# A two-layer diffusion block on one core: the first Hyena butterfly moves into the matmuls, and a third of the modulation product moves between the layers

## The chip, the cores and the metric

The kernel runs on one NeuronCore of a Trainium2 chip. The time is the device time of one execution, in microseconds; a profile of one execution goes with it. The engines are TensorE (PE; its weight loads are listed apart as PEld), VectorE (DVE), ScalarE (ACT), GpSimd (POOL) and SyncE (SP), which issues most of the transfers. Each engine runs its own instructions in order and waits on semaphores for the others.

## The reference, cut to what matters

```python
for l in range(2):                         # 1024 tokens x 1024 channels
    sh1, sc1, g1, sh2, sc2, g2 = _adaln(c, w_mod[l], b_mod[l], 6)   # silu(c) @ w_mod[l] + b_mod[l]
    hl = rmsnorm(xl, norm1_g[l]) * (1 + sc1) + sh1
    if l == 0: yl = _even_mixer(hl, ...)   # RG-LRU heads and Hyena channels
    else:      yl = _conformer_conv(hl, ...)
    xl = xl + g1 * yl
    xl = xl + g2 * _ec_moe(rmsnorm(xl, norm2_g[l]) * (1 + sc2) + sh2, ...)   # 16 experts, 128 tokens each
return rmsnorm(xl, final_g)

def hyena(v, gates):                       # 512 channels, two orders
    z = v
    for o in range(2):
        z = gates[o] * (irfft(rfft(z, 2n) * kf[o], 2n)[:n] + z * bias[o])
```

`w_mod[l]` is 1024 x 6144. Of layer 1, the first third (`sh1`, `sc1`) is wanted by the norm that opens the layer; `g1`, `sh2`, `sc2`, `g2` are wanted after its convolution.

## The kernel before, in words

A tile framework traces the program, orders each engine's instructions ahead of time by a planner (program order as the priority, its own costs for when an input will be ready), and sets the semaphores. On the chip that order is fixed: an engine, or SP's queue of transfers, that waits holds up what stands behind it.

**Stages, in the order of time.** Filters of the Hyena part; input norm and the RG-LRU part; from about 270 to 556 us the Hyena part; output projection, routing and 16 experts of layer 0 (up to about 1279 us); the conformer part of layer 1, which begins with reading the residual stream `acc` back; routing and 16 experts of layer 1.

**Hyena.** Four blocks of 128 channels, two orders each, so eight jobs. A job is a transform of length 2048 as a product with cosines and sines (`G`, 128x128 pieces, float32) for eight token residues, followed by an eight-point transform on DVE. `short` is a block of the input projection, 48 float32r matmuls of 512 columns through `mm3` (a hi/lo split), and a three-tap convolution: three for each channel block. `to_tok` transposes a signal into `ut` (token order) by 8 TensorE transposes and two ACT copies. `hy_fwd` (L593) makes 16 matmuls of 128 columns; the profile counts two records for each float32 matmul. Residues a and a+4 lie beside each other in a PSUM tile; ACT copies one of them to SBUF (`y4`, L596) and `hy_st1` forms sum and difference on DVE (L603, L604). `hy_mid` is all DVE: eight-point transform (`fft8`), product with the filter `K`, first inverse butterfly, eight-point transform back. `hy_inv` (L632) has 16 matmuls; `hy_gate` (L640) multiplies the PSUM result with the gate, reading and writing SBUF in strides of eight elements. The result of order 0 goes through `to_tok` into the job of order 1 of the same block; `X` has three buffers, `ut` two, PSUM four one-bank tiles ("n") and two two-bank tiles ("w", for `short`).

**Modulation.** `silu(c) @ w_mod` is 48 pieces of 1 MB: `ada_load` brings one into the ring `wr` (four buffers, shared with `K` and others), `ada_mm` (L229) multiplies it in four column strips, and after eight pieces `ada_end` transposes the sums (L245), adds the bias and stores rows to DRAM for later. Eight pieces are multiplied during the filters; the other 40 by `self.fill(5)` twice for each channel block, 10 pieces a block.

**Experts.** Each of 192 weight pieces of 1 MB is loaded into `wr` or the ring `wx` (12 buffers, pool `px`), split hi/lo by ACT and DVE (L158, L159) and multiplied. `moe_load` is called after each piece; when the list is empty (the last 20 calls) it does nothing. At the end of expert 15 the result is scaled (L1313) and scattered into `acc` by an indirect transfer from POOL's queue (L1314); then SP loads `acc` in eight tiles (L286) for the conformer's norm, whose outputs `hh`, `hl` lie where `wx` was.

Of the kernel before, what the change touches and what calls it, by code (L numbers as in the profile page):

```python
# [29 lines left out]

VEC = {}
_off = 0
for _n, _w in (("c", 8), ("cc", 8), ("n1g0", 8), ("n1g1", 8), ("n2g0", 8), ("n2g1", 8),
               ("bm0", 48), ("bm1", 48), ("caw", 16), ("cab", 4), ("lbr", 8), ("lbi", 8),
               ("lam", 8), ("cbw", 36), ("cbb", 12), ("fb1", 1), ("fb2", 1), ("fq", 2),
               ("cfb1", 16), ("lng", 8), ("lnb", 8)):
    if _n == "cfb1":
        NLATE = _off
    VEC[_n] = (_off, _w)
    _off += _w  # L40
NVEC = _off
NX = 12
# [7 lines left out]
def layout(inp):  # L50
# [13 lines left out]
    for l in range(2):  # L64
        put(f"n1g{l}", _cols(inp["norm1_g"][l]))
        put(f"n2g{l}", _cols(inp["norm2_g"][l]))
        put(f"bm{l}", _cols(inp["b_mod"][l]))
    put("caw", np.concatenate([_cols(inp["conv_a_w"][0][k]) for k in range(4)], 1))
    put("cab", _cols(inp["conv_a_b"][0]))
    put("lbr", _cols(inp["lru_br"][0]))  # L70
# [75 lines left out]
class Builder:  # L146
# [22 lines left out]
    def consts(self):  # L169
        nc, tc, A = self.nc, self.tc, self.A  # L170
        P, T = self.P, self.T
        self.vec = self.E.tile([128, NLATE], F32, name="vec")
        nc.sync.dma_start(self.vec, A["vec"][:, :NLATE])
        self.idn = P.tile([128, 128], F32, name="idn")
        nc.gpsimd.memset(self.idn, 0.0)
        nc.gpsimd.affine_select(self.idn, self.idn, pattern=[[-1, 128]], compare_op=OP.not_equal,
                                fill=1.0, base=0, channel_multiplier=1)
        self.stack = P.tile([128, NE], F32, name="stack")
        nc.vector.tensor_tensor(self.stack, self.idn[:, 0:NE], self.idn[:, 32:32 + NE], op=OP.add)
        for g in (64, 96):  # L180
# [24 lines left out]
        nc.vector.tensor_scalar(th, th, 0.5, 0.5, op0=OP.mult, op1=OP.add)  # L205
        self.sp = self.E.tile([128, 8, 32], F32, name="sp")
        nc.vector.memset(self.sp, 0.0)
        for i in range(2):
            nc.vector.tensor_tensor(self.sp[:, :, i], th[:, 8 * i:8 * i + 8], self.v("c", 8 * i, 8), op=OP.mult)
        self.mod = [P.tile([128, 48], F32, name=f"mod{l}") for l in range(2)]  # L210
        self.modc = P.tile([128, 16], F32, name="modc")
        self.gg = [[P.tile([128, 8], F32, name=f"gg{l}{i}") for i in range(2)] for l in range(2)]
        self.ggc = P.tile([128, 8], F32, name="ggc")

    def ada_load(self):
        if self.ada_todo:
# [5 lines left out]
    def ada_mm(self):  # L222
        if not self.ada_have:
            return
        l, s, kc, w = self.ada_have.pop(0)
        if kc == 0:
            self.ada_q = self.ps.tile([128, 512], F32, name="q", tag="n")
        for j in range(4):
            self.nc.tensor.matmul(self.ada_q[32 * j:32 * j + 32, :], self.sp[:, kc, :], w[:, j * 512:(j + 1) * 512],  # L229
                                  start=kc == 0, stop=kc == 7, tile_position=(0, 32 * j))  # L230
        if kc == 7:
            self.ada_end(l, s, self.ada_q)

    def fill(self, n=1):
        for _ in range(n):
# [2 lines left out]

    def ada_end(self, l, s, q):
        nc = self.nc  # L240
        r = self.wr.tile([128, 512], F32, name="w", tag="w")
        nc.scalar.copy(r, q)
        t = self.ps.tile([128, 512], F32, name="t", tag="n")
        for b in range(4):
            nc.tensor.transpose(t[:, b * 128:(b + 1) * 128], r[:, b * 128:(b + 1) * 128], self.idn)  # L245
        tv = t.rearrange("p (b j x) -> p j b x", b=4, j=4, x=32)
        nc.vector.tensor_tensor(self.mod[l][:, s * 16:(s + 1) * 16].rearrange("p (j b) -> p j b", j=4),
                                tv[:, :, :, 0], self.v(f"bm{l}", s * 16, 16).rearrange("p (j b) -> p j b", j=4),
                                op=OP.add)
        if l == 0 and s == 0:  # L250
            nc.vector.tensor_tensor(self.modc.rearrange("p (j b) -> p j b", j=4),
# [332 lines left out]
    def hy_fwd(self, p, J):  # L584
        nc = self.nc
        J["K"] = K = self.wr.tile([128, 8, 2, 128], F32, name="w", tag="w")
        nc.sync.dma_start(K, self.kd[J["o"]][J["qd"]])
        J["q"] = []
        for a in range(4):
            q = self.ps.tile([128, 2, 2, 128], F32, name="q", tag="n")  # L590
            for j in range(2):
                for ri in range(2):
                    nc.tensor.matmul(q[:, j, ri], self.G[:, a + 4 * j, ri * 128:ri * 128 + 128], J["u"][:, a + 4 * j],  # L593
                                     start=True, stop=True)
            y4 = p.tile([128, 2, 128], F32, name="y4", tag="y4", bufs=2)
            nc.scalar.copy(y4, q[:, 1])  # L596
            J["q"].append((q, y4))

    def hy_st1(self, p, J):
        V = self.nc.vector  # L600
        J["pq"] = pq = p.tile([128, 8, 2, 128], F32, name="pq", tag="X", bufs=3)
        for a, (q, y4) in enumerate(J["q"]):
            V.tensor_tensor(pq[:, a], q[:, 0], y4, op=OP.add)  # L603
            V.tensor_tensor(pq[:, 4 + a], q[:, 0], y4, op=OP.subtract)  # L604

    def hy_mid(self, p, J):
        V = self.nc.vector
# [27 lines left out]
    def hy_gate(self, p, J):  # L635
        dst = p.tile([128, D], F32, name="zt", tag="zt", bufs=1)
        zv = dst.rearrange("q (p a) -> q a p", a=8)
        gv = J["gate"].rearrange("q (p a) -> q a p", a=8)
        for h, q in enumerate(J["r"]):
            self.nc.vector.tensor_tensor(zv[:, h * 4:h * 4 + 4], q, gv[:, h * 4:h * 4 + 4], op=OP.mult)  # L640
        return dst

    def to_tok(self, src, dst):
        nc = self.nc
        for h in range(2):
            q = self.ps.tile([128, 4, 128], F32, name="q", tag="n")
            for j in range(4):
                a = h * 4 + j
                nc.tensor.transpose(q[:, j], src[:, a::8], self.idn)
            nc.scalar.copy(dst[:, h * 4:h * 4 + 4, :], q)  # L650

    def even_mixer(self, st, so):
        nc, tc, A = self.nc, self.tc, self.A
# [1 line left out]
        def pool(st, name, side=None):  # L655
            return st.enter_context(tc.tile_pool(name=name, bufs=1, side=side, reuse_waits="tile"))

        self.ada_todo = [(l, s_, k) for l in range(2) for s_ in range(3) for k in range(8)]
        self.ada_have = []
        with ExitStack() as s1, ExitStack() as sl:  # L660
            sl.push(self.stE.pop_all())
# [108 lines left out]
                return y  # L770

            def tok(y):
                ut = py.tile([128, 8, 128], F32, name="ut", tag="u", bufs=2)
                self.to_tok(y, ut)
                return ut

# [13 lines left out]
            for i in range(4):  # L790
                J0 = dict(o=0, qd=i, u=tok(short(i)))
                if i == 0:
                    with tc.issue_after(getattr(gload, "ins", gload)):
                        nc.sync.dma_start(self.IG, A["IG"])
                        self.fill(5)
                else:
                    self.fill(5)
                self.hy_fwd(py, J0)
                self.hy_st1(py, J0)
# [4 lines left out]
                self.fill(5)  # L804
# [4 lines left out]
                self.hy_st1(py, J1)  # L809
                self.hy_mid(py, J1)  # L810
                pend.append(J1)
            for _ in range(len(self.ada_todo) + len(self.ada_have)):
                self.fill()
            for ct in (2, 3):
                gate(py, ct, "cv", D)
            sl.close()
# [353 lines left out]

    def moe_load(self, eng=None):
        if not self.names:
            return
        n = 47 * 4 - len(self.names)
        if n % (NX + 4) < 4:
            w = self.wr.tile([128, 2, D], F32, name="w", tag="w")
# [15 lines left out]
    def experts(self, l):  # L1192
        nc, tc, A = self.nc, self.tc, self.A
        V = nc.vector
        with tc.tile_pool(name=f"pe{l}", bufs=1, side="right", reuse_waits="tile") as pe:
# [92 lines left out]
            for e in range(NE):  # L1288
# [20 lines left out]
                if l == 1 and e == NE - 1:  # L1309
# [3 lines left out]
                V.scalar_tensor_tensor(yo, y, self.gates[:, e:e + 1], g2b, op0=OP.mult, op1=OP.mult)  # L1313
                self.last = nc.gpsimd.indirect_dma_start(self.acc[l][:, :], bass.IndirectOffsetOnAxis(ap=xT[e][1][:, 0:1], axis=0),  # L1314
                                             yo, None, compute_op=OP.add)

    def conformer(self, st):
        nc, tc, A = self.nc, self.tc, self.A
# [324 lines left out]
```

## Time and profile before

| | |
|---|---|
| median of 3 runs | 2297.8 us (2295.29 to 2300.59) |
| profiled execution, its own time | 2297.13 us |
| span of its profile | 2295.1 us |
| mean granted TensorE clock | 0.962 of full speed |
| busy share of the span | PE 93%, DVE 79%, ACT 52%, POOL 6% |
| transfers | 616.13 MB, 268 GB/s over the span |

Busy PE time is modelled and overlaps from one matmul to the next, so 93% is no measure of free room; the idle time before an instruction, and what ended it, is. The chain of waits follows the work that ended last back from the end of the span.

### The profile page before, as it was taken

To read this page: it belongs to the slowest core of one execution; us is meant where nothing else is said; L and a number is where in the kernel's file an instruction comes from. 1 tells how busy PE (TensorE), PEld (TensorE's weight loads), DVE (VectorE), ACT (ScalarE), POOL (GpSimd) and SP (SyncE) were. 2 spreads that over 40 slices of the span, in tenths; PEclk is the share of its full clock that TensorE was granted. 3 is DMA by queue.
4 is the path that set the end of the run, shared out by engine and by line. 5 is a ranking of instruction groups with operands and counts; after the bars stand their busy time and mean duration, and the time that the engine had idled before them with its cause. 6 is when DMAs were issued, how large, how long until landed. Compare 5 with 4: busy or idle time off the path is not lost.

```text
span 2295.1 us, 29201 instructions
## 1 busy us (share of the span) xinstructions
PE 2123.7 (93%) x10882; PEld 1654.9 (72%) x10882; DVE 1819.8 (79%) x2876; ACT 1201.7 (52%) x1458; POOL 127.1 (6%) x128
## 2 busy tenths in 40 slices
PE   7999998996968999999999699979689999999997
PEld 5976766775745877877878488867457777777775
DVE  5979799998596988989888533276968898888887
ACT  3658511212214777777777521134247667676774
POOL 0000000000001000000000100010010000000001
PEclk9999999998988999999999899979789999999999
DMA  7241585564848999999998345234779999999974
GB/s 277 107 138 47 198 296 196 220 254 150 291 171 323 368 393 378 379 388 376 391 378 267 105 131 163 93 128 177 257 291 360 384 367 386 368 372 380 365 270 156
DMA packets 210023, 616.13 MB, mean 268 GB/s; under 512 B 27988, under 2 KB 76758, under 8 KB 200089
## 3 DMA queue, kind: packets, MB, share of 16 engines
q1 hardware_dynamic: 198634, 572.85, 66.3%
q0 software_dynamic: 11248, 41.42, 7.2%
q8 instruction: 85, 1.39, 0.2%
q14 instruction: 56, 0.46, 0.1%
HBM read 558.62 MB, written 55.61 MB: 268 GB/s over the span
## 4 chain that ended last, share of the span: by engine, by line
PE 77%; DVE 14%; DMA 3%; issue 3%; ACT 2%; POOL 1%; SPq 0%; POOLq 0%; ACTq 0%; DVEq 0%
PE P L153 20%; PE P L155 20%; PE P L154 19%; PE P L1251 6%; PE q L1216 2%; PE q L593 1%; PE q L229 1%; PE q L394 1%; PE q L510 1%; PE q L632 1%; PE q L1381 1%; PE q L307 1%; POOL rs L278 1%; DVE mm L873 0%; DMA xs<-h2d,ix 0%
## 5 line engine op out<-in xcount | busy, mean ns | idle before, releaser
L159 DVE TENSOR_TENSOR e<-wx,e 128x1024 fp32r<-128x1024 f32 x516 | 619.0, 1221 | 93.1 <-ACT e L158 78.5
L158 ACT CAST e<-wx 128x1024 fp32r<-128x1024 f32 x516 | 539.8, 1051 | 233.9 <-PE P L155 232.1
L153 PE MATMUL P<-e,th 128*128 128x512 f32 x1384 | 562.8, 407 | 0.2 <-ACT th L158 0.2
L155 PE MATMUL P<-e,tl 128*128 128x512 f32 x1384 | 543.5, 393 | 1.6 <-DVE tl L159 1.6
L154 PE MATMUL P<-e,th 128*128 128x512 f32 x1384 | 543.0, 392 | 0.0
L153 PEld LDWEIGHTS P<-e,th 128*128 128x128 f32 x1384 | 260.0, 188 | 61.6 <-issue 7.2
L154 PEld LDWEIGHTS P<-e,th 128*128 128x128 f32 x1384 | 260.1, 188 | 61.0 <-DVE e L159 4.3
L155 PEld LDWEIGHTS P<-e,tl 128*128 128x128 f32 x1384 | 259.7, 188 | 61.5 <-DVE tl L159 2.5
L159 DVE TENSOR_TENSOR e<-w,e 128x1024 fp32r<-128x1024 f32 x176 | 211.8, 1221 | 49.2 <-ACT e L158 29.6
L153 PE MATMUL P<-hh,wh 128*128 128x512 f32 x576 | 229.0, 399 | 7.9 <-DVE y L769 4.2
L158 ACT CAST e<-w 128x1024 fp32r<-128x1024 f32 x176 | 184.1, 1051 | 94.2 <-PE P L155 76.1
L154 PE MATMUL P<-hl,wh 128*128 128x512 f32 x576 | 228.1, 396 | 0.8 <-DVE ms L276 0.8
L155 PE MATMUL P<-hh,wlo 128*128 128x512 f32 x576 | 227.6, 395 | 0.0
L153 PEld LDWEIGHTS P<-hh,wh 128*128 128x128 f32 x576 | 108.8, 189 | 40.4 <-issue 13.2
L154 PEld LDWEIGHTS P<-hl,wh 128*128 128x128 f32 x576 | 109.0, 189 | 28.1 <-issue 5.1
L155 PEld LDWEIGHTS P<-hh,wlo 128*128 128x128 f32 x576 | 108.5, 188 | 27.0 <-issue 4.8
L1314 POOL DMA_INDIRECT acc<-yo,ix x31 | 50.6, 1634 | 934.7 <-DVE yo L1313 934.7
L159 DVE TENSOR_TENSOR tl<-q,th 128x512 fp32r<-128x512 f32 x128 | 84.6, 683 | 7.1 <-ACT th L158 5.1
L158 ACT CAST wh<-w 128x1024 fp32r<-128x1024 f32 x16 | 16.7, 1049 | 136.6 <-PE P L154 124.1
L1251 PE MATMUL P<-wx,xf 128*128 128x512 f32 x176 | 79.1, 592 | 0.0
L158 ACT CAST th<-q 128x512 fp32r<-128x512 f32 x128 | 71.7, 586 | 1.9 <-PE q L1216 1.9
L278 POOL TENSOR_TENSOR rs<-ms,nh 128x1 f32<-128x1 f32 x42 | 23.9, 570 | 830.1 <-issue 435.2
(406 smaller groups left out, 3057.8 us busy)
## 6 DMA issues: line engine op xcount, KB each, us to landing
wx<-i_exp_w SPq DMA_DIRECT2D x272, 1024.0 KB, 7.9
w<-i_exp_w SPq DMA_DIRECT2D x96, 1024.0 KB, 8.1
w<-i_w_mod SPq DMA_DIRECT2D x48, 1024.0 KB, 7.2
wst<-i_w_in SPq DMA_DIRECT2D x20, 512.0 KB, 3.9
kd<-w SPq DMA_DIRECT2D x8, 1024.0 KB, 5.0
w<-kd SPq DMA_DIRECT2D x8, 1024.0 KB
acc<-res SPq DMA_DIRECT2D x16, 512.0 KB, 3.0
e<-i_exp_w SPq DMA_DIRECT2D x16, 512.0 KB, 7.2
```

The lines of the kernel that those rows point to most:

```text
L153: t.matmul(o, lh, rh, start=start, stop=False)
L154: t.matmul(o, lh, rl, start=False, stop=False)
L155: t.matmul(o, ll, rh, start=False, stop=stop)
L158: self.nc.scalar.copy(hi, src)
L159: self.nc.vector.tensor_sub(lo, src, hi.bitcast(F32))
L229: self.nc.tensor.matmul(self.ada_q[32 * j:32 * j + 32, :], self.sp[:, kc, :], w[:, j * 512:(j + 1) * 512], start=kc == 0, stop=kc == 7, ti ...
L278: nc.gpsimd.tensor_tensor(r, m, self.nh[:, :n], op=OP.pow)
L307: nc.tensor.transpose(q[:, t * 128:(t + 1) * 128], x[:, c * 128:(c + 1) * 128], self.idn)
L394: nc.tensor.matmul(q[:, j], h2[:, a + j], ws[:, o, i, cs], start=True, stop=True)
L1216: nc.tensor.transpose(q[:, j], src[:, c * 128:(c + 1) * 128], self.idn)
L1251: nc.tensor.matmul(P[:, ns], f[:, k], h[:, ns], start=k == 0, stop=k == 7)
L1314: self.last = nc.gpsimd.indirect_dma_start(self.acc[l][:, :], bass.IndirectOffsetOnAxis(ap=xT[e][1][:, 0:1], axis=0), yo, None, compute_op ...
```

## The change

1. `hy_st1` and `y4` go. `to_tok` also writes the negative of residues 4 to 7 (one more ACT instruction); `ut` grows from 8 to 12 residues and has one buffer instead of two. `hy_fwd` now makes sum and difference inside PSUM: each matmul has 256 columns, the first with the residue a repeated (stride 0), the second with a+4 and its negative; ACT copies the four PSUM tiles whole to `pq`.
2. `hy_gate` copies the PSUM result by ACT into token order (strided writes), then DVE multiplies it with the gate in one contiguous 128x1024 instruction.
3. The last 16 of the modulation's 48 pieces (layer 1, thirds 1 and 2) leave the Hyena part (`fill(3)` instead of `fill(5)`). They are loaded into `wx` by the `moe_load` calls that did nothing, and multiplied after expert 15 of layer 0. Small vectors move between pools for that.

```diff
-        self.modc = P.tile([128, 16], F32, name="modc")
+        self.sp1 = P.tile([128, 8], F32, name="sp1")
+        nc.vector.tensor_copy(self.sp1, self.sp[:, :, 0])
+        self.modc = self.E.tile([128, 16], F32, name="modc")
...
     def ada_mm(self):
+        sp = self.sp1[:, kc:kc + 1].to_broadcast([128, 32]) if l and s else self.sp[:, kc, :]
         for j in range(4):
-            self.nc.tensor.matmul(self.ada_q[32 * j:32 * j + 32, :], self.sp[:, kc, :], w[:, j * 512:(j + 1) * 512],
+            self.nc.tensor.matmul(self.ada_q[32 * j:32 * j + 32, :], sp, w[:, j * 512:(j + 1) * 512],
...
+    def ada_late(self):
+        if self.moe_l or not self.ada_todo:
+            return
+        l, s, kc = self.ada_todo.pop(0)
+        w = self.px.tile([128, 2048], F32, name="wx", tag="wx", bufs=NX)
+        self.nc.sync.dma_start(w, self.A["w_mod"][l, kc * 128:(kc + 1) * 128, s * 2048:(s + 1) * 2048])
+        self.ada_have.append((l, s, kc, w))
...
     def hy_fwd(self, p, J):
-        J["q"] = []
+        J["pq"] = pq = p.tile([128, 8, 2, 128], F32, name="pq", tag="X", bufs=3)
+        u = J["u"]
         for a in range(4):
             q = self.ps.tile([128, 2, 2, 128], F32, name="q", tag="n")
-            for j in range(2):
-                for ri in range(2):
-                    nc.tensor.matmul(q[:, j, ri], self.G[:, a + 4 * j, ri * 128:ri * 128 + 128], J["u"][:, a + 4 * j],
-                                     start=True, stop=True)
-            y4 = p.tile([128, 2, 128], F32, name="y4", tag="y4", bufs=2)
-            nc.scalar.copy(y4, q[:, 1])
-            J["q"].append((q, y4))
-    def hy_st1(self, p, J):
-            V.tensor_tensor(pq[:, a], q[:, 0], y4, op=OP.add)
-            V.tensor_tensor(pq[:, 4 + a], q[:, 0], y4, op=OP.subtract)
+            for ri in range(2):
+                rs = slice(ri * 128, ri * 128 + 128)
+                nc.tensor.matmul(q[:, :, ri], self.G[:, a, rs], u[:, a:a + 1].to_broadcast([128, 2, 128]),
+                                 start=True, stop=False)
+                nc.tensor.matmul(q[:, :, ri], self.G[:, a + 4, rs], u[:, a + 4:a + 9:4], start=False, stop=True)
+            nc.scalar.copy(pq[:, a:a + 5:4], q)
...
     def hy_gate(self, p, J):
         for h, q in enumerate(J["r"]):
-            self.nc.vector.tensor_tensor(zv[:, h * 4:h * 4 + 4], q, gv[:, h * 4:h * 4 + 4], op=OP.mult)
+            self.nc.scalar.copy(zv[:, h * 4:h * 4 + 4], q)
+        self.nc.vector.tensor_tensor(dst, dst, J["gate"], op=OP.mult)
...
     def to_tok(self, src, dst):
             nc.scalar.copy(dst[:, h * 4:h * 4 + 4, :], q)
+            if h:
+                nc.scalar.activation(dst[:, 8:12, :], q, AF.Identity, bias=0.0, scale=-1.0)
...
-                ut = py.tile([128, 8, 128], F32, name="ut", tag="u", bufs=2)
+                ut = py.tile([128, 12, 128], F32, name="ut", tag="u", bufs=1)
...
-                self.fill(5)          # twice for each channel block
+                self.fill(3)
...
+            self.ada_todo = [(1, s_, k) for s_ in (1, 2) for k in range(8)]   # after the Hyena part
...
     def moe_load(self, eng=None):
         if not self.names:
-            return
+            return self.ada_late()
...
     def experts(self, l):             # after the last expert
+            if l == 0:
+                while self.ada_have or self.ada_todo:
+                    self.ada_late()
+                    self.ada_mm()
```

## Rows read from the trace of the kernel before

**Rows 1.** Windows of the Hyena part: us, busy time (instructions) by engine, clock, DMA.
```profile
268.00:530.00 262.00, 247.50 (x1467) 178.42 (x1466) 236.76 (x421) 50.73 (x81) 0.00 (x0) 0.99 0.66 243
...
360.00:378.00 18.00, 10.26 (x59) 4.28 (x58) 18.00 (x29) 2.51 (x3) 0.00 (x0) 0.81 0.54 184
...
530.00:556.00 26.00, 8.03 (x39) 6.98 (x40) 21.54 (x30) 9.28 (x8) 0.00 (x0) 0.67 0.59 205
```
**Rows 2.** Waits of PE, 268 to 530 us: total, times, longest.
```profile
PE P L153 <- DVE y L769: 4.2, 1, 4.2
PE q L229 <- DMA w<-i_w_mod: 2.6, 2, 1.4
...
PE q L265 <- DVE mod L247: 1.4, 1, 1.4
```
**Rows 3.** Groups by shape, 265 to 560 us: busy us, mean ns, idle before.
```profile
L640 DVE TENSOR_TENSOR zt<-q,y 128x512 f32<-128x512 f32 x16 | 17.9, 1128 | 10.0 <-PE q L632 9.9
...
L603 DVE TENSOR_TENSOR pq<-q,y 128x256 f32<-128x256 f32 x32 | 13.4, 418 | 18.3 <-ACT y L596 17.7
...
L619 DVE TENSOR_TENSOR pq<-pq,sub 128x1024 f32<-128x1024 f32 x8 | 9.8, 1219 | 0.0
...
L650 ACT COPY ut<-q 128x512 f32<-128x512 f32 x16 | 9.1, 588 | 46.5 <-PE q L649 46.5
```
**Rows 4.** Groups by shape of PE, 150 to 240 us: float32 matmuls of two widths.
```profile
L510 PE MATMUL q<-xa,bd 128*128 128x512 f32 x64 | 30.3, 594 | 0.0
...
L510 PE MATMUL q<-xa,bd 128*128 128x256 f32 x32 | 9.9, 389 | 1.5 <-DVE xa L498 1.5
```
**Rows 5.** Chain that ended last, 440 to 480 us: start, us, what.
```profile
455.86 2.71 PE q L229 x24
...
467.20 0.44 PE t L245 x4
...
476.07 1.00 PE q L229 x8
```
**Rows 6.** Groups by shape of ACT, 0 to 25 us: strided, then contiguous writes.
```profile
L330 ACT ACTIVATE h<-sx 64x512 f32<-64x512 f32 x2 | 2.2, 1117 | 2.6 <-DVE sx L327 2.6
...
L330 ACT ACTIVATE h<-sx 128x512 f32<-128x512 f32 x1 | 0.6, 631 | 3.7 <-DVE sx L327 3.7
```
**Rows 7.** Chain that ended last, 512 to 556 us, the end of the Hyena part.
```profile
516.26 3.63 PE q L593 x32
...
521.12 0.60 DVE sub L565
...
534.10 2.05 issue
...
537.36 2.20 DVE ol L971
```
**Rows 8.** Windows at the end of layer 0's experts, columns as in rows 1.
```profile
1238.00:1244.00 6.00, 6.00 (x28) 4.97 (x27) 5.67 (x7) 4.86 (x6) 0.00 (x0) 1.00 0.07 18
1244.00:1262.00 18.00, 18.00 (x81) 14.93 (x80) 16.81 (x15) 14.40 (x15) 2.28 (x1) 1.00 1.12 257
1262.00:1279.00 17.00, 14.64 (x66) 11.21 (x65) 12.12 (x18) 7.98 (x9) 0.00 (x0) 1.00 0.00 0
1279.00:1293.00 14.00, 0.18 (x1) 0.00 (x0) 4.17 (x5) 4.29 (x6) 2.12 (x2) 0.62 0.62 170
1293.00:1303.00 10.00, 7.40 (x27) 5.36 (x28) 5.94 (x14) 7.22 (x13) 3.06 (x5) 0.51 1.04 359
```
**Rows 9.** Chain that ended last, 1276 to 1303 us.
```profile
1280.79 6.32 DMA acc<-yo,ix
...
1290.03 9.43 DMA x<-acc
```
**Rows 10.** Matmuls writing PSUM in two runs: chain, 640 to 705 us, and a window.
```profile
692.23 0.76 PE pre L1129 x7
...
690.00:694.00 4.00, 1.61 (x17) 1.30 (x17) 2.31 (x11) 0.00 (x0) 0.00 (x0) 0.50 1.03 410
```

More of the change, by code (lines that the diff above doesn't have):

```diff
@@ L32 @@
 _off = 0
-for _n, _w in (("c", 8), ("cc", 8), ("n1g0", 8), ("n1g1", 8), ("n2g0", 8), ("n2g1", 8),
-               ("bm0", 48), ("bm1", 48), ("caw", 16), ("cab", 4), ("lbr", 8), ("lbi", 8),
+for _n, _w in (("c", 8), ("cc", 8), ("n1g0", 8), ("n1g1", 8), ("n2g0", 8),
+               ("bm0", 48), ("bm1", 16), ("caw", 16), ("cab", 4), ("lbr", 8), ("lbi", 8),
                ("lam", 8), ("cbw", 36), ("cbb", 12), ("fb1", 1), ("fb2", 1), ("fq", 2),
-               ("cfb1", 16), ("lng", 8), ("lnb", 8)):
+               ("cfb1", 16), ("lng", 8), ("lnb", 8), ("bl1", 32), ("n2g1", 8)):
     if _n == "cfb1":
@@ L66, in layout @@
         put(f"n2g{l}", _cols(inp["norm2_g"][l]))
-        put(f"bm{l}", _cols(inp["b_mod"][l]))
+        b = _cols(inp["b_mod"][l])
+        put(f"bm{l}", b[:, :16] if l else b)
+        if l:
+            put("bl1", b[:, 16:])
     put("caw", np.concatenate([_cols(inp["conv_a_w"][0][k]) for k in range(4)], 1))
@@ L209, in consts @@
             nc.vector.tensor_tensor(self.sp[:, :, i], th[:, 8 * i:8 * i + 8], self.v("c", 8 * i, 8), op=OP.mult)
+        self.sp1 = P.tile([128, 8], F32, name="sp1")
+        nc.vector.tensor_copy(self.sp1, self.sp[:, :, 0])
         self.mod = [P.tile([128, 48], F32, name=f"mod{l}") for l in range(2)]
-        self.modc = P.tile([128, 16], F32, name="modc")
+        self.modc = self.E.tile([128, 16], F32, name="modc")
         self.gg = [[P.tile([128, 8], F32, name=f"gg{l}{i}") for i in range(2)] for l in range(2)]
-        self.ggc = P.tile([128, 8], F32, name="ggc")
+        self.ggc = self.E.tile([128, 8], F32, name="ggc")
     def ada_load(self):
@@ L240, in ada_end @@
         nc = self.nc
-        r = self.wr.tile([128, 512], F32, name="w", tag="w")
+        if l and s:
+            r = self.px.tile([128, 2048], F32, name="wx", tag="wx", bufs=NX)[:, :512]
+        else:
+            r = self.wr.tile([128, 512], F32, name="w", tag="w")
         nc.scalar.copy(r, q)
+        bm = self.v("bl1", s * 16 - 16, 16) if l and s else self.v(f"bm{l}", s * 16, 16)
         t = self.ps.tile([128, 512], F32, name="t", tag="n")
@@ L247, in ada_end @@
         nc.vector.tensor_tensor(self.mod[l][:, s * 16:(s + 1) * 16].rearrange("p (j b) -> p j b", j=4),
-                                tv[:, :, :, 0], self.v(f"bm{l}", s * 16, 16).rearrange("p (j b) -> p j b", j=4),
+                                tv[:, :, :, 0], bm.rearrange("p (j b) -> p j b", j=4),
                                 op=OP.add)
@@ L587, in hy_fwd @@
         nc.sync.dma_start(K, self.kd[J["o"]][J["qd"]])
-        J["q"] = []
+        J["pq"] = pq = p.tile([128, 8, 2, 128], F32, name="pq", tag="X", bufs=3)
+        u = J["u"]
         for a in range(4):
             q = self.ps.tile([128, 2, 2, 128], F32, name="q", tag="n")
-            for j in range(2):
-                for ri in range(2):
-                    nc.tensor.matmul(q[:, j, ri], self.G[:, a + 4 * j, ri * 128:ri * 128 + 128], J["u"][:, a + 4 * j],
-                                     start=True, stop=True)
-            y4 = p.tile([128, 2, 128], F32, name="y4", tag="y4", bufs=2)
-            nc.scalar.copy(y4, q[:, 1])
-            J["q"].append((q, y4))
-    def hy_st1(self, p, J):
-        V = self.nc.vector
-        J["pq"] = pq = p.tile([128, 8, 2, 128], F32, name="pq", tag="X", bufs=3)
-        for a, (q, y4) in enumerate(J["q"]):
-            V.tensor_tensor(pq[:, a], q[:, 0], y4, op=OP.add)
-            V.tensor_tensor(pq[:, 4 + a], q[:, 0], y4, op=OP.subtract)
+            for ri in range(2):
[4 more added lines that the diff above has]
+            nc.scalar.copy(pq[:, a:a + 5:4], q)
     def hy_mid(self, p, J):
@@ L637, in hy_gate @@
         zv = dst.rearrange("q (p a) -> q a p", a=8)
-        gv = J["gate"].rearrange("q (p a) -> q a p", a=8)
         for h, q in enumerate(J["r"]):
-            self.nc.vector.tensor_tensor(zv[:, h * 4:h * 4 + 4], q, gv[:, h * 4:h * 4 + 4], op=OP.mult)
+            self.nc.scalar.copy(zv[:, h * 4:h * 4 + 4], q)
+        self.nc.vector.tensor_tensor(dst, dst, J["gate"], op=OP.mult)
         return dst
@@ L656, in pool @@
             return st.enter_context(tc.tile_pool(name=name, bufs=1, side=side, reuse_waits="tile"))
-        self.ada_todo = [(l, s_, k) for l in range(2) for s_ in range(3) for k in range(8)]
+        self.ada_todo = [(l, s_, k) for l, s_ in ((0, 0), (0, 1), (0, 2), (1, 0)) for k in range(8)]
         self.ada_have = []
@@ L794, in even_mixer @@
                         nc.sync.dma_start(self.IG, A["IG"])
-                        self.fill(5)
+                        self.fill(3)
                 else:
-                    self.fill(5)
+                    self.fill(3)
                 self.hy_fwd(py, J0)
-                self.hy_st1(py, J0)
                 if pend:
@@ L803, in even_mixer @@
                 J0["gate"] = short(4 + i)
-                self.fill(5)
+                self.fill(3)
                 g1 = short(8 + i)
```

1 line of the change is left out of this document (removed).

## The prediction

> **What bounds it now.** I read the page first: PE is busy 93% of the span, DVE 79%, and the chain that ended last lies 77% on PE. That is an average over stages, so the two places that the change touches are read by themselves.
>
> In the Hyena part (268 to 530 us) the windows show PE busy 247.5 of 262 us and DVE 236.8 [rows 1]. Both are nearly full. The reader is to see that PE's own waits there are few: 4.2 us behind the convolution of `short`, 1.4 us in `ada_end` [rows 2], and, from 360 to 378 us, a stretch in which DVE is busy throughout and PE 10.3 of 18 us at a granted clock of 0.81 [rows 1]. That stretch costs 7.7 us of idle and 18 x 0.19 = 3.4 us of clock, so over half of the 14.5 idle us, and the loss of clock, 11 us together, sit in one place, where DVE is late. Elsewhere PE sets the pace. From 530 to 556 us it turns round: DVE is busy 21.5 of 26 us, PE 8.0, and the chain goes through the last job, with two splits of the output weights (2.05 us shown as issue, then 2.20) standing in it [rows 7].
>
> Between the layers the windows show PE idle from 1279 to 1293 us, DMA idle from 1262 to 1279, and from 1293 to 1303 a PE clock of 0.51 while the DMA share is 1.04 [rows 8]. The chain runs through the scatter (6.32 us) and then the reading back of `acc` (9.43 us) [rows 9]: the loads of `x` set the start of layer 1.
>
> **The change part by part.**
>
> *Doubled columns in `hy_fwd` (PE, a loss).* 16 matmuls, 32 records, go from 128 to 256 columns. The trace has 256 and 512 columns in float32: 389 and 594 ns, so 205/256 = 0.80 ns a column and 0.103 us for 128 more [rows 4]. A job's 3.63 us [rows 7] becomes 3.63 + 32 x 0.103 = 6.9, +3.3 us; eight jobs +26, of which 23 before the last job and 3.3 in it. The new matmuls write PSUM in two runs of 128 columns, which no float32 row shows. The nearest are the seven bfloat16 matmuls of L1129, 896 columns in two runs each: 0.76 us at a clock of 0.50, i.e. 1.2 GHz, and 896/1.2 = 0.75 us [rows 10], full pace. I take no price; the other bound is a rival.
>
> The Trainium skill (SBUF — State Buffer, "Door 1: The DMA port swizzle") says that any non-contiguous pattern in PSUM slows matmuls significantly. It speaks against the change. The row of the two-run matmuls does not bear it out, at runs as short as 16 columns; by the rule the sum would be that of the last rival.
>
> *Modulation out of the Hyena part (PE, a gain).* Three pieces in a row take 2.71 us, one alone 1.00 [rows 5]: 0.90 to 1.00 each, 16 pieces 14.5 to 16; I take 15. Two `ada_end` go too, 0.44 us of transposes [rows 5] and up to 1.4 of waiting [rows 2] each, the last of them beside the tail: 1 us. Their 16 transfers leave the ring `wr`; PE waited 2.6 us in all for such transfers [rows 2], so that gains nothing I count.
>
> *DVE relief.* L603 and L604, 64 instructions at 0.42 us [rows 3], go: 27 us. `hy_gate`: 16 x 1.13 go, 8 x 1.22 come [rows 3], -8. Together up to 35 of 237 us; neighbours on DVE overlap at their ends, so it may be some us less. Where PE sets the pace this is worth nothing; where DVE is late it is worth the 11 us above. I take 10.
>
> *New latency.* From the middle of a block's order 0 to that of order 1, the chain gets: the copy of the gate. A 512-column ACT write in strides takes 1.12 us against 0.63 contiguous [rows 6], so 0.59 to 1.12; nearest to the new form is the strided one. Then 0.1 us more of multiply (1.22 against the last half's 1.13), 0.59 for the negative [rows 3], and 3.3 of matmul; the trailing DVE sums (521.12 less the 519.9 at which the matmuls end, 1.2 us [rows 7]) become one ACT copy, 0.6: -0.6. That is +4.5 a block. With one `ut` buffer the next block's copy waits for the matmuls too. `short` and the other work on both engines cover it in the later blocks; in the first, with little ready, I charge 3 us net (0 to 7).
>
> So before the last job: +23 - 15 - 1 - 10 + 3 = 0.
>
> *The tail.* In the last job nothing covers the 4.5 us. Against that, DVE arrives with less behind it, so the two splits of 2 us each may leave the chain: I count half, -2. Tail +2.5 (0 to +5). Hyena in all +2, rounded.
>
> *The pieces between the layers.* PE: 16 x 0.90 to 1.00 = 15 us of matmul against 14 us of idle and a following 10 at half clock [rows 8]; with this cover it costs nothing, without it 15. DMA: `wx` gives four buffers early, eight as expert 15's pieces are split, and the last four only after the first four pieces have been multiplied, behind the last expert, after 1279 us. At 359 GB/s [rows 8] a piece takes 1.05 MB/359 = 2.9 us; twelve are 35 us, and the 18 us of conformer weights [rows 8] share the time. The experts' last weights are in before 1238, where DMA stands still (share 0.07 [rows 8]); from about 1234 the sum ends at 1287. The last four, 11.7 us, then land at about 1295 to 1299, or 1291 if the others are in at 1279. SP's queue issues the loads of `x` at 1287, when the scatter has landed (1280.79 + 6.32 [rows 9]), behind them. They come some 5 us later than now (4 to 12, 1291 or 1299 less 1287); what waits for them is the norm, hence all of layer 1. The `hl` buffers also lie where the last pieces were, but those are multiplied by then. On the other side, PE is kept at work and its clock may stand at 2.4 GHz instead of 1.2 GHz from 1293 to 1303, where it is busy 7.4 of 10 us; since `x` sets the pace I count 1 to 2 us. Net +4 (bounds 0, all landed in time, and +12, the last pieces and `x` one after the other).
>
> Sum: 2297.1 (the profiled execution's own time) + 2 + 4 = 2303.1; that execution stands 0.7 under the median, so 2304.
>
> **The rivals.**
>
> *DVE sets the Hyena part (faster).* The mid parts on DVE follow one another with hardly a gap, and PE's full look comes from modulation and gate blocks that fill its waits. Then the 35 us count until PE binds: stalls go entirely (-14.5 in place of -10, the first block's +3 covered), the splits leave the tail (-4.3 in place of -2): -10 to the forecast's +2. With the layers at +1 to +4 the time is 2288 to 2291. It decides where PE's extra 7 us (23 - 15 - 1) stay under the idle time that they find. For it: DVE's 18.0 of 18 at 360. Against: PE's few waits elsewhere.
>
> *PE binds in full.* The stall is replaced by another, since the planner's order is made anew and 7 us more stand on PE: no -10, or the first block's 7: Hyena +10, time 2312.
>
> *The transfers collide.* The +12 of the layers comes: 2312. For it: the four last buffers come free only at 1279. Against: DMA idles 17 us before.
>
> *Runs in PSUM slow the matmuls.* If the pace of 0.80 ns a column halved, 32 x 8 x 0.205 = 53 us more: about 2357. Only the rule speaks for it.
>
> **How the numbers follow.** Forecast 0.40, spread 2298 to 2310; DVE rival 0.32; PE binds 0.14; transfers 0.11; PSUM 0.03. A measurement can tell about 0.2%, 4.6 us, from no change: faster is under 2293.2, slower over 2302.4. Faster takes 0.28 of the DVE rival; same the other 0.04 and 0.16 of the forecast; slower 0.24 of the forecast and 0.28 of the rest. The likeliest gives 2304. To leave out no more than 2 in 10 the range runs from 2286, the foot of the DVE rival, to 2317, above the two at 2312.
>
> **What would show it.** In the profile after: L-lines of `hy_fwd` near 389 ns mean for 256 columns and 6.9 us a job; the stretch from the first modulation matmul to the last job's start as long as before, with DVE's share down to near 0.78 and no stretch like 360 to 378; the last job some 4 us longer on PE; the first `x` landing after 1293 and PE busy with modulation from 1279. Wrong it would be if PE's idle time in the Hyena part does not fall, or falls with DVE's work to nothing; if modulation matmuls stand in PE's order before data that is late, inside expert 15; or if `x` lands as before.

## The result, and the profile after

The changed kernel takes 2321.2 us (median of 4 runs, 2318.75 to 2324.31) beside 2298.7 of the kernel before (4 runs on the same chip): a ratio of 1.0099, 95% interval 1.0087 to 1.0111. It is slower by 22.5 us. The forecast of 2304 had the direction, but the time lies above its range. The profiled execution's span is 2318.0 us at a clock of 0.962, 22.9 longer than that of before at the same clock.

Windows of the Hyena part of the kernel after, columns as in [rows 1]:

```profile
268.00:530.00 262.00, 249.39 (x1293) 191.32 (x1293) 201.61 (x340) 73.06 (x97) 0.00 (x0) 0.97 0.49 178
360.00:378.00 18.00, 14.06 (x68) 9.19 (x61) 16.53 (x26) 0.82 (x1) 0.00 (x0) 0.81 0.71 264
530.00:556.00 26.00, 15.26 (x70) 13.06 (x69) 24.25 (x33) 10.01 (x8) 0.00 (x0) 0.78 0.52 180
```

DVE is down to 201.6 of 262 us, as forecast, and PE is as busy as before, but the stretch from 360 us still stands at a clock of 0.81. Groups by shape of the same part, beside [rows 3]:

```profile
L612 PE MATMUL q<-ut,G 128*128 128x256 f32 x128 | 37.4, 385 | 0.1
L614 PE MATMUL q<-ut,G 128*128 128x256 f32 x128 | 36.7, 380 | 0.0
...
L615 ACT COPY pq<-q 128x512 f32<-128x512 f32 x32 | 18.7, 586 | 46.7 <-PE q L614 46.7
L650 ACT COPY zt<-q 128x512 f32<-128x512 f32 x16 | 17.7, 1137 | 50.7 <-PE q L643 47.1 <-issue 3.5
L651 DVE TENSOR_TENSOR zt<-zt,y 128x1024 f32<-128x1024 f32 x8 | 9.8, 1226 | 10.0 <-ACT zt L650 10.0
```

The doubled matmuls take 380 to 385 ns, as the 389 of an unbroken write of the same width [rows 4]. The gates' copies take 1.14 us, as the strided writes of [rows 6].

Windows from the end of expert 15 to layer 1, beside [rows 8]:

```profile
1247.00:1265.00 18.00, 18.00 (x81) 14.89 (x80) 16.81 (x15) 14.39 (x15) 2.28 (x1) 1.00 0.45 132
1265.00:1282.00 17.00, 14.64 (x69) 11.19 (x71) 11.14 (x12) 7.74 (x9) 0.00 (x0) 1.00 0.97 366
1282.00:1296.00 14.00, 13.03 (x118) 3.80 (x110) 1.40 (x2) 0.95 (x2) 1.55 (x1) 1.00 0.95 321
1296.00:1306.00 10.00, 2.94 (x23) 0.92 (x20) 2.06 (x2) 2.47 (x3) 0.00 (x0) 0.82 1.13 313
1306.00:1316.00 10.00, 1.10 (x5) 0.23 (x3) 1.60 (x11) 1.57 (x4) 0.00 (x0) 0.50 0.81 250
1316.00:1326.00 10.00, 7.08 (x27) 5.07 (x27) 5.93 (x14) 8.01 (x15) 3.67 (x6) 0.50 1.07 372
```

PE multiplies the pieces from 1282 to 1296, as forecast, but then stands nearly still for 20 us, and its clock is at 0.50 (1.2 GHz) when layer 1 begins. In the chain that ended last stands what it waits for (start, us, what; the work in between is left out):

```profile
1281.90 7.05 PE q L235 x64
1288.97 0.59 ACT wx L259
1289.61 0.67 PE t L263 x4
1291.01 0.37 ACT wx L285
1291.39 0.29 SPq L286
1291.74 0.39 SPq L1354
1292.17 10.59 DMA w<-i_cf_w
...
1303.82 1.04 ACT wh L161
1304.86 0.49 ACT wx L259
1305.39 1.13 PE t L263 x4
1307.75 0.37 ACT wx L285
1308.14 0.29 SPq L286
1308.53 0.52 SPq L1367
1309.10 0.59 SPq L1367
1309.79 4.80 DMA x<-acc
1314.67 1.16 ACT junk L307 x2
```

Read downwards: the row store of third 1 (L286) waits for that third's eight pieces. Behind it on SP's queue stand the conformer's weights (L1354). They land 10.6 us later. ACT, in order, casts them (L161) before it copies third 2 out of PSUM (L259), though its matmuls had ended at 1300.3. So the second row store comes at 1308.1, and behind it `x` at 1309.8. In the kernel before, `x` went out at 1287.26.

The first measure used below for this stretch runs from the issue of the last scatter to the first use of `x` (ACT's squares for the norm). It was 1290.54 less 1280.79, **9.8 us**; it is 1314.67 less 1283.50, **31.2 us**: +21.4. For the Hyena part the measure is from the first start of `hy_fwd` that the trace has to that of the last job: 236.3 before, 238.7 now, +2.4. From the last job to the scatter it is 764.7 and 766.7. The first job starts 1.8 us earlier than before, and what follows the first use of `x` is 1.2 shorter.

The first use of `x` is not yet the start of layer 1's work. A second measure therefore runs from the same issue of the scatter to the first matmul of layer 1, which multiplies the norm's output (`hh`): 19.3 us before, 39.9 after, +20.6. What follows that matmul takes 993.3 to 995.1 us in all the kernels below but e2 (997.3), while what follows the first use of `x` ranges from 1002.4 to 1009.1. Where the two measures differ, the second says more of the time of the whole kernel.

### The profile page after: what moved, and what is told of

It is laid out like the page before. It is cut to its first block, busy times and chain, and to the rows that moved or that the text cites. A ratio compares the mean times of both kernels' runs of the same rounds, so it can differ in the third digit from the quotient of the medians.

```text
span 2318.0 us, 29136 instructions
## 1 busy us (share of the span) xinstructions
PE 2150.9 (93%) x10882; PEld 1678.3 (72%) x10882; DVE 1791.2 (77%) x2805; ACT 1229.3 (53%) x1482; POOL 126.9 (5%) x128
## 4 chain that ended last, share of the span: by engine, by line
PE 80%; DVE 11%; DMA 3%; issue 3%; ACT 2%; POOL 1%; SPq 0%; POOLq 0%; ACTq 0%; DVEq 0%
PE P L156 20%; PE P L158 20%; PE P L157 20%; PE P L1263 6%; PE q L1228 2%; PE q L235 1%; PE q L612 1%; PE q L528 1%; PE q L614 1%; PE q L643 1%; PE q L412 1%; DMA wx<-i_exp_w 1%; PE q L1397 1%; PE q L325 1%; POOL rs L296 1%
## 5 line engine op out<-in xcount | busy, mean ns | idle before, releaser
L161 ACT CAST e<-wx 128x1024 fp32r<-128x1024 f32 x516 | 539.9, 1051 | 233.8 <-PE P L158 233.3
L161 ACT CAST e<-w 128x1024 fp32r<-128x1024 f32 x176 | 183.8, 1050 | 94.9 <-PE P L158 76.2
L161 ACT CAST wh<-w 128x1024 fp32r<-128x1024 f32 x16 | 16.7, 1049 | 135.6 <-PE P L157 124.1
L161 ACT CAST th<-q 128x512 fp32r<-128x512 f32 x128 | 71.7, 586 | 1.9 <-PE q L1228 1.9
```

The source lines that it names most:

```text
L161: self.nc.scalar.copy(hi, src)
```

## The experiments

Every kernel was timed beside the kernel before on its chip (4 to 10 runs each; the median of before was 2296.3 to 2299.1 on these chips, so the ratios are what compares). H is the Hyena measure, S the one between the layers to the first use of `x`, and N the one to the first matmul of layer 1; each is from one profiled execution.

| run | us | ratio to before | H | S | N |
|---|---|---|---|---|---|
| before | 2298.7 | 1 | 236.3 | 9.8 | 19.3 |
| after | 2321.2 | 1.0099 [1.0087, 1.0111] | 238.7 | 31.2 | 39.9 |
| e1, row stores on POOL's queue | 2317.5 | 1.0090 [1.0061, 1.0119] | 237.9 | 30.2 | 38.9 |
| e2, conformer's weights early | 2314.6 | 1.0078 [1.0052, 1.0104] | 238.9 | 23.8 | 33.5 |
| e3, both | 2313.4 | 1.0080 [1.0052, 1.0107] | 238.5 | 20.8 | 30.8 |
| e4, pieces back in the Hyena part | 2308.4 | 1.0049 [1.0034, 1.0064] | 246.1 | 10.2 | 19.3 |
| e9, e3 with half the bytes | 2308.4 | 1.0039 [1.0021, 1.0056] | 238.8 | 15.3 | 29.6 |
| e10, after with half the bytes | 2312.4 | 1.0060 [1.0043, 1.0076] | 238.5 | 25.1 | 33.7 |
| e11, e3 with 8 late pieces | 2309.6 | 1.0054 [1.0034, 1.0074] | 238.5 | 11.8 | 21.0 |
| e5, late pieces alone | 2311.3 | 1.0053 [1.0034, 1.0072] | 231.0 | 31.6 | 40.3 |
| e6, radix step alone | 2308.8 | 1.0045 [1.0028, 1.0062] | 246.8 | 10.0 | 19.7 |
| e7, gates alone | 2303.3 | 1.0026 [1.0016, 1.0037] | 240.7 | 10.6 | 19.7 |
| e13, e5 mended, 8 late pieces | 2297.7 | 1.0002 [0.9991, 1.0012] | 235.2 | 11.8 | 21.0 |
| e14, e11 with the other 8 spread | 2300.2 | 1.0008 [0.9999, 1.0018] | 235.5 | 11.8 | 21.0 |

**First: order or bytes?** Theory 1 was that `x` is late because of what stands in front of it in in-order queues; theory 2, that 16 MB more simply take the DMA engines' time. Three runs change the order and move the same bytes; a fourth takes the pieces back.

```diff
# e1
-            nc.sync.dma_start(self.rowd[l]...
+            (nc.gpsimd if l else nc.sync).dma_start(self.rowd[l]...
# e2, in ada_late; the conformer takes these three instead of loading its own
+        if len(self.ada_todo) <= 12 and len(self.cf_pre) < 3:
+            self.cf_load((0, 4, 1)[len(self.cf_pre)])
# e3: both.  e4: all 48 pieces in the Hyena part, fill(5)
-        self.ada_todo = [(l, s_, k) for l, s_ in ((0, 0), (0, 1), (0, 2), (1, 0)) for k in range(8)]
+        self.ada_todo = [(l, s_, k) for l in range(2) for s_ in range(3) for k in range(8)]
```

> Row stores of layer 1's late modulation issued from POOL's queue in place of SP's; nothing else differs from the changed kernel. Theory 1 (the queue: x waits in SP's order behind two row stores, and these behind a chain over ACT): the x loads no longer wait for the rows, so they issue some 15 us earlier, at about 1292 to 1295 instead of 1309.8, right behind the conformer's weights; time 2308 to 2312. Theory 2 (the bytes: 16 pieces, the conformer's weights and x take the DMA engines' time in any order): x lands when it did, time within 3 us of 2321. The conformer's weights stand behind the pieces as before, so ACT's cast of them still lands at about 1303 under both.

> The first three weights of the conformer are issued after the first four late pieces instead of after all sixteen; the row stores stay on SP's queue. Theory 1: the weights land before 1290, the cast on ACT no longer holds up the copy of the late modulation that stands behind it, the second row store issues some 6 us earlier (about 1302) and x behind it: time 2312 to 2316. Theory 2 (bytes): within 3 us of 2321.

> Both: conformer's weights early and the row stores on POOL's queue. Theory 1: x issues as soon as the scatter has landed, at about 1290, and lands some 2 to 5 us later than in the kernel before for the pieces still under way; of the 20.6 us between the layers 3 to 6 are left, time 2302 to 2306. Theory 2 (bytes): within 3 us of 2321, since the same bytes move.

> The changed kernel with all 48 modulation pieces multiplied in the Hyena part again; the radix step in PSUM and the gates by copies stay. Both theories: the stretch between the layers is as in the kernel before (-20.6). Then the Hyena part carries 15 us of matmul more: +15 if PE sets it in full (2316), +5 if a third of it fills waits (2305). If the time stays at 2321 the loss is not the pieces'.

e1 missed: S fell by 1.0, not 15. The row stores alone were not what held `x`: without them it issues 24.2 us after the scatter's issue, with them 26.3. Timeline of SP's queue in e1 (start, us, instruction, count), then its durations for the conformer's weights, and those of the kernel before:

```profile
1283.00 18.73 SPq L1354 DMA_DIRECT2D w<-i_cf_w  x6
1301.82 2.60 SPq L1367 DMA_DIRECT2D dwb<-i_dwb  x2
1304.53 5.28 SPq L304 DMA_DIRECT2D x<-acc  x8
```
```profile
L1354 SPq DMA_DIRECT2D w<-i_cf_w x16: 372/1507/9199, 1283.0 to 1400.5; - x16
```
```profile
L1338 SPq DMA_DIRECT2D w<-i_cf_w x16: 368/681/5406, 1242.1 to 1380.4; - x16
```

With nothing in front of them but the last pieces, the six loads of the conformer's weights keep SP itself for 18.7 us, one of them for 9.2 (the three numbers are least, median and longest, in ns). In the kernel before, the first eight took from 1242.1 to 1254.1, under expert 15. So theory 1 as I had put it falls in its place, not in its kind: the weights, not the rows, are what `x` chiefly stands behind; the rows come next. e2 takes the weights away and S falls by 7.4, and its time of 2314.6 lies in the expected range; `x` then stands behind the first row store. The way there was not the expected one: ACT's cast of the early weights still comes before the copy of the late modulation, since it starts only when the scatter has landed (1294.4; the scatter's issue at 1283.2 and 11.0 us). e3 takes both away: S falls by 10.4 and N by 9.1. But it was expected to reach 2302 to 2306, and stands at 2313: of S 11.0 us are still left, of N 11.5. Theory 2 in full falls by these measures too: the same bytes moved, and layer 1 began 9 us sooner after the scatter. By the times alone it does not fall, since the intervals of e3 and of the changed kernel overlap.

In e3 the chain and SP's timeline show the 11.0 of S:

```profile
1283.03 10.71 DMA acc<-yo,ix
```
```profile
1293.79 9.32 SPq L312 DMA_DIRECT2D x<-acc  x8
```

The scatter takes 10.7 us instead of 6.3 [rows 9], with pieces on the same engines: `x` issues 10.8 us after the scatter's issue, before 6.5. And the first `x` is used 10.0 us after its issue, before 3.3. That is 4.3 + 6.7 = 11.0. This suggested a theory A: with the order mended, what is left is bytes.

e4 shows the other side: with the pieces back in the Hyena part S is 10.2 and N as before, so the loss between the layers is the pieces' alone; and H is +9.8.

**Then: are the 11 us bytes?** Half of each late piece is left out (half of those modulation columns), with the same number of matmuls and instructions, once with the order mended and once without; or 8 of the pieces go back. Theory B is that another in-order queue holds the rest.

```diff
# e9 (on e3), e10 (on the changed kernel)
-        self.nc.sync.dma_start(w, self.A["w_mod"][l, kc * 128:(kc + 1) * 128, s * 2048:(s + 1) * 2048])
+        self.nc.sync.dma_start(w[:, :1024], self.A["w_mod"][l, kc * 128:(kc + 1) * 128, s * 2048:s * 2048 + 1024])
...
+            jw = j % 2 if l and s else j          # columns 0 to 1023 multiplied twice
# e11 (on e3; the conformer's weights after 2 late pieces); e14 with fill(4) besides
-            self.ada_todo = [(1, s_, k) for s_ in (1, 2) for k in range(8)]
+            self.ada_todo = [(1, 2, k) for k in range(8)]
```

> The kernel with both mendings of the order (conformer's weights early, row stores on POOL's queue), and each late piece loaded with only 1024 of its 2048 columns, multiplied twice over: half of the late pieces' bytes, the same matmuls, waits and instructions. It leaves out half of the modulation's columns for gates 1 and norm 2 of layer 1. Theory A (with the order mended, what is left of the loss is bytes: scatter and x share the DMA engines with the last pieces): the scatter lands in about 6.5 us again instead of 10.8, the first x is read about 3.5 us after its issue instead of 10, and the time falls by 7 to 10 us, to 2303 to 2306. Theory B (what is left is still a place in some in-order queue): the time stays at 2310 to 2314.

> The changed kernel, order untouched, with half of the late pieces' bytes in the same way (half of those modulation columns left out). Theory A with the queue (x behind the second row store): the pieces land sooner, so the first row store and the conformer's weights behind it come some 5 us sooner, but x still waits for the second row store behind ACT's cast of these weights: x issues at 1298 to 1302 instead of 1309.8, time 2309 to 2314. Bytes alone: x issues at about 1290, time 2300 to 2304. Queue alone: 2319 to 2323.

> Both mendings, and only the last 8 pieces late (norm 2 of layer 1); the other 8 are multiplied in the Hyena part. Theory A (bytes): 8.4 MB fewer behind expert 15, of the 11 us left between the layers 2 to 4 remain; the Hyena part carries 8 pieces more, about half of the 7.4 us that 16 pieces cost there: time 2308 less 1 to 5, about 2306 to 2311. Theory B: 2313 to 2318.

The four values make a square:

| us | S, all bytes | S, half | N, all bytes | N, half |
|---|---|---|---|---|
| order as changed | 31.2 | 25.1 | 39.9 | 33.7 |
| order mended | 20.8 | 15.3 | 30.8 | 29.6 |

By S order and bytes seem to add: the order is worth 10.4 and 9.8, half of the bytes 6.1 and 5.5. By N they do not: the order is worth 9.1 with all bytes and 4.1 with half, and half of the bytes 6.2 with the order as changed and only 1.2 with it mended. So in e9 `x` comes sooner, but layer 1 hardly starts sooner. Its first matmul in the kernel before, the changed one, e10, e3 and e9, from the timelines (N is its start less the scatter's issue at 1280.79, 1283.50, 1285.21, 1283.03 and 1285.62):

```profile
1300.06 1.22 PE L153 MATMUL P<-hh,wh 128*128 128x512 f32 x2 [0.23 <-ACT hh L313]
1323.36 1.22 PE L156 MATMUL P<-hh,wh 128*128 128x512 f32 x2 [0.23 <-ACT hh L331]
1318.95 0.79 PE L156 MATMUL P<-hh,wh 128*128 128x512 f32 x1 [0.23 <-ACT hh L332]
1313.83 0.73 PE L156 MATMUL P<-hh,wh 128*128 128x512 f32 x2 [0.54 <-ACT hh L339]
1315.20 0.73 PE L156 MATMUL P<-hh,wh 128*128 128x512 f32 x2 [1.15 <-ACT hh L340]
```

The reason stands in the chains of e3 and of e9 (e9's last row is cut by the window, the 64 matmuls end at 1309.5):

```profile
1294.91 1.04 ACT wh L161
1295.95 0.49 ACT wx L267
1296.49 1.13 PE t L271 x4
1297.87 0.59 PE q L291 x2
1298.46 8.73 PE q L235 x64
1307.21 0.59 ACT wx L267
```
```profile
1296.99 1.03 ACT wh L161
1298.02 0.49 ACT wx L268
1298.56 1.13 PE t L272 x4
1299.94 0.59 PE q L292 x2
1300.53 8.52 PE q L236 x57
```

The two mendings moved the hold-up from SP's queue to ACT's. The cast of the early weights (`wh`) starts 0.2 us after the scatter has landed, in e3 and in e9. Behind it ACT copies third 1 out of PSUM, and behind that copy PE, idle for 8.0 us in e3 and 7.5 in e9, does third 1's transposes and only then the matmuls of third 2. ACT copies third 2 before the squares of the later tiles of `x`, and waits for it: 5.2 us in e9. In e10, where the weights come late, ACT copies third 1 at 1290.7, before the cast, and third 2's matmuls end at 1299.6. So theory B holds for much of what is left, with ACT's queue as the place; theory A holds at most for the scatter, which takes 10.7 us in e3, still 10.2 in e9, and 6.6 when only 8 pieces are late (e11). Of the 11.5 us of N left in e3, 4.4 are the scatter's and 7.1 lie between the cast and the first matmul. No run takes the 7.1 away with 16 late pieces; that they are ACT's order is read from the trace and not shown by a run.

The times separate less than the traces. As ratios to before they put half of the bytes at 0.4% (9 us) with either order, and the order at 0.2% (4 to 5 us) with all bytes or half. Only the halving with the order as changed (e10) is clear of noise; the other three pairs of intervals overlap. e3's profile is of an execution of 2309.7 us (median 2313.4), e9's of one of 2311.9 (median 2308.4). So how the loss divides between order and bytes is known only roughly. e9's median lies 2.4 us above its expected range. e10's time is in the range of theory A with the queue, though its `x` issued at 1305.6, later than expected.

With eight late pieces (e11) they have landed before the scatter is issued (no DMA traffic from 1286 to 1293 us, the scatter at 1293.1), S is 11.8, 2.0 over before, and N 21.0, 1.7 over. Its time was within the expected range, but for a wrong reason: I had left the piece count of `fill` at 3, so the eight pieces that went back all stood behind the last job, and from there to the scatter it took 775.9 us instead of 766.7. e14, below, mends that.

**The parts by themselves**, each on the kernel before:

```diff
# e5: the 16 late pieces, radix step and gates as before
-                self.fill(5)
+                self.fill(3)
# e6: hy_fwd of the changed kernel, gates and 48 pieces as before
# e7: hy_gate of the changed kernel, radix step and 48 pieces as before
```

> The kernel before with only the 16 late pieces moved; radix step and gates on DVE as before. The loss between the layers is the same +20.6; what the pieces' leaving gives the Hyena part is -7.4 if it is what it was between the changed kernel and the one with the pieces back, -15 if PE sets that part in full, 0 if DVE does: time 2309, 2302 or 2317.

> Only the radix-2 step in PSUM by TensorE; the gates on DVE, all 48 pieces in the Hyena part. Theory P (PE sets the pace; DVE's relief is worth only what PE waited): 26 us of matmul more, some 10 of them given back: the first job to the last takes +8 to +14, time 2307 to 2313. Theory D (DVE sets it): 27 us of adds off DVE, the stretch shortens, time 2285 to 2295.

> Only the gates in token order by ScalarE copies; the radix step on DVE, all 48 pieces in the Hyena part. Theory P: 8 us of DVE work off, one copy of 0.6 to 1.1 us more in the chain of a job: -3 to +3, time 2296 to 2302. Theory D: -6 to -8, time 2290 to 2293. If the loss of the two parts together (the run with the pieces back) is the copies' wait and not the wider matmuls, this run is +6 to +10.

The late pieces alone lose 21.8 between the layers and give 5.3 in the Hyena part: 2311.3. The radix step alone costs 10.5 in H although it takes 27 us of adds from DVE; windows of e6, then of e7:

```profile
268.00:530.00 262.00, 253.74 (x1388) 182.87 (x1388) 204.68 (x335) 57.20 (x83) 0.00 (x0) 0.99 0.65 240
```
```profile
268.00:530.00 262.00, 243.80 (x1448) 176.03 (x1447) 224.85 (x409) 64.87 (x94) 0.00 (x0) 0.97 0.64 238
```

In e6 PE is full (253.7 of 262, before 247.5) and DVE is not (204.7, before 236.8): PE sets the pace, and theory D is out. The stretch from 360 to 378 us, where PE had been busy 10.3 of 18 us at a clock of 0.81, is full in e6 (17.8 us, at 1.00): there the relief of DVE did what the prediction said. The gates alone cost 4.4 in H and 5.1 us in time, a little above the expected range and short of the +6 to +10 by which the copies would have been the whole loss, with DVE relieved and PE less busy at a lower clock. That speaks for the copies' added wait; which wait it is, no run singles out. Together they cost 9.8 in H (e4), less than 10.5 + 4.4.

**The mended versions:**

> The kernel before with 8 late pieces in place of 16 (4 instead of 5 pieces at a time in the Hyena part), conformer's weights early and row stores on POOL's queue. Between the layers +2 as in the run of the changed kernel with eight late pieces; the Hyena part gains half of the 5.9 us that it gained by 16: time -1 against the kernel before, 2294 to 2299. If the Hyena part gains only where the last pieces were, 0 gain: 2300 to 2302.

> The changed kernel with both mendings and 8 late pieces, and the other 8 spread over the Hyena part (4 pieces at a time instead of 3), where the run before it left them for after the last job. Theory: the 10 us that those 8 pieces cost there become 3.7 (half of what 16 cost spread): 2303 to 2306. If they cost their full 7 us of matmul wherever they stand: 2308 to 2311.

e13 is level with the kernel before: what 8 pieces give (1.1 in H) is lost between the layers (2.0). e14, the whole change with the order mended and half of the late pieces, is level too (its interval ends at 1.0018, where the changed kernel's begins at 1.0087). It is also better than expected. Windows of the changed kernel, then of e14:

```profile
420.00:440.00 20.00, 14.67 (x59) 10.25 (x58) 19.48 (x31) 2.01 (x3) 0.00 (x0) 0.83 0.63 228
```
```profile
360.00:378.00 18.00, 18.00 (x85) 13.63 (x78) 17.97 (x28) 2.15 (x2) 0.00 (x0) 1.00 0.38 136
420.00:440.00 20.00, 20.00 (x103) 13.16 (x96) 19.82 (x30) 3.97 (x4) 0.00 (x0) 1.00 0.62 234
```

With three pieces at a time PE is busy 14 to 15 us in each of these two windows, and the granted clock is 0.81 and 0.83. With four pieces the same windows are full at 1.00 (2.4 GHz), and eight pieces *more* in the Hyena part make H 3.0 us *shorter* than with e11's arrangement (235.5 to 238.5). That pieces fill PE's waits where DVE is late fits this pair, but it is no rule. With five at a time (e4) the windows are as full (17.6 of 18 and 20.0 of 20 us, at 1.00), and H is 246.1. Without the radix step and the gates' copies H rises with the pieces: 231.0, 235.2 and 236.3 with three, four and five (e5, e13, before). The planner orders every kernel anew, and no run changes the number of pieces with the order held fixed, so the cause of the 3.0 us stays open. No version beat the kernel before.

## Why the prediction was wrong

**The step that failed** is "The pieces between the layers": +4, bounds 0 and +12, measured +21.4. Its PE part held: PE multiplied the pieces where it had been idle (13.0 of 14 us from 1282). Its landing held as well: the last pieces were forecast at 1295 to 1299, and PE waits for the last until 1299.2. What was wrong is the next sentence, by which SP's queue "issues the loads of `x` at 1287, when the scatter has landed". I counted the conformer's weights as bytes that share the time, and not as six instructions on SP's queue. Before, they are issued while SP has nothing else; after the change they stand behind all 16 pieces and the first row store, whose own data is ready only when eight pieces have been multiplied. The list that was needed is: everything that SP issues between its old place under expert 15 and `x`. With that order mended (e3), 10.4 of the 21.4 us go, by N 9.1 of 20.6. Of the 11.5 of N that stay, 4.4 are the scatter, which the pieces slow (10.7 us against 6.3) and which I had taken as unchanged; the other 7.1 lie in ACT's and PE's order behind it, where the late modulation and the conformer's cast stand in one another's way. The value taken, +4, had neither the two orders nor the slower scatter.

The bound of +12 priced only the landing of the last pieces and `x`, and so was no bound of the sum. The rival "The transfers collide" named the right place, with the same 12; it too left the order of the queues out.

**The gain of the clock** (1 to 2 us) did not come: PE stood idle again before `x` landed, and the window from 1316 is at 0.50.

**The Hyena part**, +2 forecast: 2.4 by H, and from the last job to the scatter 2.0 more; the first job starts 1.8 earlier, so that the scatter is issued 2.7 later. That the sum came near is luck. With all pieces kept, the parts of PE and DVE come to +9.8 (e4) where +16 was forecast (23 - 10 + 3); taking the pieces out then gave 7.4 where 16 was (15, and 1 for `ada_end`). The two errors nearly cancel. The terms:
- *Doubled columns*, 6.9 us a job: 32 records from 516.77 to 523.94 in the chain of the last job, 7.2. The rule of the Trainium skill (SBUF — State Buffer, "Door 1: The DMA port swizzle"), by which non-contiguous patterns in PSUM slow matmuls, is not borne out by the 380 to 385 ns above. Together with the relief of DVE, +13 in the forecast (23 - 10), they are +10.5 in e6.
- *Modulation out*, -15: -7.4 (after less e4) and -5.3 (e5). The step treated all pieces as work that only takes PE's time. In the changed form the first eight to go gave 10.6 (e4 to e14) and the second eight cost 3.0; in the form before the first gave 1.1 and the second 4.2 (before, e13, e5). Why they differ, no run shows.
- *DVE relief*, -10 for the stretch at 360: seen in e6 and e4, where PE fills it (17.8 and 17.6 of 18 us, at 1.00), but not in the changed kernel. There PE is busier (14.1 us, before 10.3) but still at 0.81, and a second such stretch appears at 420. The sum had counted the relief and the pieces' leaving as if neither changed the other.
- *New latency*, +3: the gates alone are +4.4, near it, but the sum had the latency of both parts, so this is no test of it.
- *Tail*, +2.5: from the last job's start to the scatter it is 2.0 more. But e13, without the radix step and the gates' copies, takes as long there (767.0, before 764.7, after 766.7), so no run ties the 2.0 to the tail.

**Against the rivals:** DVE does not set the Hyena part; e6 decides it. That rival's sum was also off: by its own terms (23 - 15 - 1 - 14.5, then 4.5 - 4.3) its Hyena part is about -7, and its time some 3 us above the 2288 to 2291 stated. "PE binds in full" asked for +10 in the Hyena part, which came to 2.4; with all pieces kept its terms give +26 (23 + 3), and e4 has 9.8. "Runs in PSUM slow the matmuls" falls by the 380 to 385 ns.

## What to carry to other kernels

When transfers move to another place in an in-order queue, write down every instruction that the queue issues between the new place and the load that sets the end, also those of the next stage that used to go out early, and what each of them waits for; bytes and buffers are only half of the price. Ask the same of what lands beside them: here a scatter on the path took 4 us longer for the company. Go through the other engines' orders as well: mending SP's queue brought `x` sooner, and then ACT's order held layer 1. Measure to the first work that needs everything, here the first matmul, and not to the first use of one input. And small work among an engine's waits is not worth its own length when taken away: 15 us of it gave 5 to 7, and giving half of it back made the stage 3 us shorter in one form of the kernel and 4 us longer in the other.

## What the runs showed of the hardware that I had not expected

- Issuing a load can hold the issuing engine: of the loads of 512 KB of the conformer's weights (runs of 512 bytes in memory) one took SP 0.37 us at the least and 9.2 at the most, right behind the late pieces; the median over the kernel is 0.68 us before and 1.5 in e1. The Trainium skill (Perfetto Trace Analysis, "What “DMA-bound” means") takes a solid row of transfers on the issuing engine for the making of descriptors. The row of 18.7 us in e1 fits that; but one load of the same shape took 0.37 us and another 9.2, which suggests that what is already under way counts too. No run separates the two.
- The scatter with accumulation took 6.3 to 6.4 us with no late piece still under way (before; e14) and 10.7 beside such transfers (e3); halving the others' bytes hardly helped it (`x` issues 10.2 us after the scatter's issue in e9, 10.8 in e3).
